# A diffusion trunk on one core: the first layer's feed-forward split into all latents, then the context, with the latents' projections behind the second sweep

## The chip, the cores and the metric

The kernel runs on one NeuronCore of a Trainium2 chip. The metric is the device time of one execution in microseconds (us). Engines are named as in the profile: PE is the matrix engine (PEld its weight loads), DVE the vector engine, ACT the scalar engine, POOL GpSimd, SP the engine that issues the weight transfers.

## The reference

Two layers over 1024 latent tokens and 256 context tokens, 1024 features, all in 32-bit floats. Layer 0 mixes tokens with a convolution module, layer 1 with grouped-query attention (16 query heads, 4 key heads, head size 64, normed q and k, rotary positions on latents). Each layer ends in a SwiGLU feed-forward of width 2816. Only latents are returned, so the last layer does not update the context.

```python
for i in range(DEPTH):                      # DEPTH = 2
    hx = rmsnorm(x, norm_g[i, 0]) * (1.0 + sc_x) + sh_x      # the same for ctx -> hc
    # i == 0: yx, yc = conv_module(hx), conv_module(hc)
    # i == 1: yx = attention over the keys of hx and hc
    x = x + g_x * rmsnorm(yx, norm_g[i, 1])
    fx = rmsnorm(x, norm_g[i, 2]) * (1.0 + scf_x) + shf_x
    x = x + gf_x * rmsnorm(swiglu(fx, ffn_w1[i], ffn_w3[i], ffn_w2[i]), norm_g[i, 3])
    # layer 0 alone does the last three lines for ctx, too
```

The shifts, scales and gates (`sh`, `sc`, `g`) come from six linear maps per layer of silu(c) for latents and of silu(c_ctx) for the context.

## The kernel before

Features lie on the 128 partitions, tokens in the columns. Tokens are cut into three pieces: C (256 context columns), L and R (512 latent columns each). A matmul of full precision is three matmuls on split halves: `mm3` (L154 to L156) multiplies weights' high part with both halves of the input and weights' low part with its high half. `wload` brings a weight tile of 512 KB into one of two landing buffers (`wr`), ACT casts the high part (`wh`, L131), DVE subtracts the low part (`wl`, L135; on POOL, L137, while `lo_dve` is 0); of each of these there are three buffers. Scratch comes from small rings: `sm` (3 buffers), `sb` (4), `acc` (2).

`ffn` walks over 22 tiles of the hidden width in groups of four (the last of two). For each, `up` loads the tiles of w1 and w3, multiplies all pieces of the call with them, and forms silu(a) * b (L646, L647) as two halves in a ring of five slots (`hrs`); one tile into the next group, `down` multiplies the group before with w2 and adds the result to y on DVE (L671). While the feed-forward is written down, `pump` takes steps of generators waiting in `bgq` (the background), each step with a cost, half a us of background for each nominal us of matmuls. The order thus written is a priority: within it each engine gets an instruction early or late as its inputs are expected, and each engine then runs its own list in order.

Around the change, the order before is:

- post-norms of the convolution (`pp`, a `post_pre`: sum of squares, scale, add to the residual, store as `x1d`, second norm into the halves `fv`) for C and L, then the convolution's last projection of R;
- a sweep of `ffn(0, ...)` over C and L; behind it R's `pp` and `mods`. The latter computes the modulation of layer 1: `mod_half` loads 112 chunks of 256 KB into four buffers and reduces each on DVE against one or two conditioning rows (L264). Its conditioning rows and buffers share one allocation (`HR`) with C's y;
- a sweep over R alone; behind it (`early`) the closing norms (`final`, which stores `x2d`) of C and L, layer 1's input norm of C, C's keys and values, and the input norm of L;
- `qkv` of L, `final` and `norm_in` of R, `qkv` of R. `qkv` projects K, V and four pairs of query tiles. `qk_pair` takes squares of both tiles of a pair on ACT, adds them on DVE (L715), sums each head by small matmuls (L719), takes reciprocal roots on DVE, rotates, splits and stores four parts (`ksd`, eight transfers for a K pair; `qsd`, four for a query pair);
- `attention`: a first pass of 16 units (4 key heads, 4 query blocks of L). A unit has scores (24 matmuls, L816), their scaling (L822) and exponentials, then transposes and the product with V (L834 to L841), one unit behind. R's query projections run in the background of its first units; meanwhile scores use one region of PSUM, and later two;
- the output projection of L with the second pass (R's query blocks) in the background, and layer 1's feed-forward.

## Time and profile before

| what | value |
|---|---|
| median of 3 runs | 3094.52 us (3092.87 to 3094.85) |
| profiled execution | 3094.26 us |
| its span, first to last instruction | 3092.0 us |
| mean granted PE clock | 0.969 |
| busy: PE, DVE, ACT, POOL | 2906.2, 1926.1, 1195.9, 264.6 us |
| HBM read, written | 289.76 MB, 41.81 MB |

In a row of a group of instructions stand line, engine, operation, output and inputs, shape and count; then busy us and the mean ns of one, then idle time of the engine before them with what ended it. A row of waits reads: who waited for whom, us in total, times, longest. A row of transfers has the count, KB each, and the median us from issue to landing. "in" names tensors in memory; lower-case and capital names are the program's tiles (`T` stands for T1 to T6).

### The profile page before, as it was taken

The page shows a single profiled execution, that of the slowest core. Times are in us where ns is not written, and L with a number is a line of the kernel's source. Part 1 is how long each engine was busy: PE and PEld are TensorE (multiplying, and loading weights), DVE is VectorE, ACT ScalarE, POOL GpSimd, SP SyncE. Part 2 cuts the span into 40 slices and gives each one's busy share as a digit, 9 for nine tenths or more (in the row PEclk, how much of TensorE's full clock was granted, in tenths as well). Part 3 has the DMA queues.
Part 4 walks back from the last instruction along what each step waited for, and adds up shares of the span by engine and source line. Part 5 has one row for each costly group of instructions (what it writes and reads, how often), then busy time and mean ns, then how long its engine had stood idle before and what let it go on. Part 6 is the DMA issues. An engine that isn't in the chain of part 4 may idle for free. (4 is left out here: it accounts for less than half of the span.)

```text
span 3092.0 us, 38855 instructions
## 1 busy us (share of the span) xinstructions
PE 2906.2 (94%) x14890; PEld 2416.0 (78%) x14890; DVE 1926.1 (62%) x3400; ACT 1195.9 (39%) x1880; POOL 264.6 (9%) x416
## 2 busy tenths in 40 slices
PE   7899969998999999999958899989999999999997
PEld 5788858887888887888846678767777778788886
DVE  5886777898533366433565899766566653743335
ACT  5222255421121134222333688645555543332222
POOL 0000001123100011000113211110000000100000
PEclk9999979999999999999979999989999999999999
DMA  6542424367312234333345311222222232443232
GB/s 234 148 126 68 134 87 140 140 198 234 127 62 65 65 116 137 109 96 96 118 145 154 96 64 43 86 79 75 67 83 78 67 121 95 150 131 95 95 95 75
DMA packets 143322, 339.58 MB, mean 110 GB/s; under 512 B 41888, under 2 KB 63392, under 8 KB 141984
## 3 DMA queue, kind: packets, MB, share of 16 engines
q1 hardware_dynamic: 76432, 221.94, 22.3%
q0 software_dynamic: 40592, 107.06, 11.1%
q10 hardware_dynamic: 26112, 8.10, 1.1%
q8 instruction: 117, 1.92, 0.3%
q14 instruction: 69, 0.57, 0.1%
HBM read 289.76 MB, written 41.81 MB: 107 GB/s over the span
## 5 line engine op out<-in xcount | busy, mean ns | idle before, releaser
L156 PE MATMUL ps<-T,wl 128*128 128x512 f32 (+1 forms) x2256 | 847.7, 377 | 22.8 <-DVE wl L135 22.8
L154 PE MATMUL ps<-T,wh 128*128 128x512 f32 (+1 forms) x2256 | 849.5, 377 | 13.1 <-ACT T L143 4.9
L155 PE MATMUL ps<-T,wh 128*128 128x512 f32 (+1 forms) x2192 | 822.3, 375 | 1.0 <-DVE T L146 0.7
L131 ACT CAST wh<-wr 128x1024 fp32r<-128x1024 f32 x348 | 365.4, 1050 | 1049.4 <-PE ps L155 774.6
L135 DVE TENSOR_TENSOR wl<-wr,wh 128x1024 fp32r<-128x1024 f32 x340 | 415.8, 1224 | 390.8 <-ACT wh L131 385.7
L156 PEld LDWEIGHTS ps<-T,wl 128*128 128x128 f32 x2256 | 430.3, 191 | 100.8 <-DVE wl L135 25.5
L154 PEld LDWEIGHTS ps<-T,wh 128*128 128x128 f32 x2256 | 430.4, 191 | 91.1 <-ACT T L143 6.4
L155 PEld LDWEIGHTS ps<-T,wh 128*128 128x128 f32 x2192 | 418.4, 191 | 74.7 <-DVE T L146 2.0
L155 PE MATMUL ps<-HS,wh 128*128 128x512 f32 (+1 forms) x784 | 306.4, 391 | 0.0
L838 DVE TENSOR_TENSOR T<-ps,T 128x512 fp32r<-128x512 f32 x320 | 216.8, 687 | 110.2 <-ACT T L837 108.9
L154 PE MATMUL ps<-HS,wh 128*128 128x512 f32 (+1 forms) x720 | 280.9, 392 | 0.0
L156 PE MATMUL ps<-HS,wl 128*128 128x512 f32 (+1 forms) x720 | 280.6, 390 | 0.0
L837 ACT CAST T<-ps 128x512 fp32r<-128x512 f32 x320 | 186.2, 586 | 182.9 <-PE ps L834 164.5
L834 PE MATMUL ps<-cst,T 128*128 128x128 f32 x1100 | 193.3, 277 | 17.7 <-DVE T L838 17.3
L671 DVE TENSOR_TENSOR T<-ps,T 128x512 f32<-128x512 f32 (+1 forms) x168 | 110.7, 664 | 146.0 <-PE ps L156 145.3
L822 DVE TENSOR_SCALAR_CACHE_REDUCE T<-ps,rq 128x1280 f32<-128x1280 f32 x110 | 169.9, 1545 | 29.2 <-PE ps L816 24.6
L834 PEld LDWEIGHTS ps<-cst,T 128*128 128x128 f32 x1100 | 133.8, 142 | 65.3 <-DVE T L838 45.5
L647 DVE TENSOR_TENSOR sm<-sm,ps 128x256 f32<-128x256 f32 (+1 forms) x88 | 54.5, 620 | 197.4 <-PE ps L156 197.3
L824 ACT ACTIVATE T<-T,mn 128x1280 f32<-128x1280 f32 x110 | 150.4, 1367 | 66.4 <-DVE T L822 64.5
L155 PEld LDWEIGHTS ps<-HS,wh 128*128 128x128 f32 x784 | 149.2, 190 | 29.0 <-DVE HS L146 0.2
L816 PE MATMUL ps<-KB,q 128*128 128x512 f32 (+1 forms) x576 | 144.6, 371 | 20.5 <-DMA KB<-ksd 13.0
L156 PEld LDWEIGHTS ps<-HS,wl 128*128 128x128 f32 x720 | 136.8, 190 | 27.7
(212 smaller groups left out, 4207.4 us busy)
## 6 DMA issues: line engine op xcount, KB each, us to landing
wr<-in_w SPq DMA_DIRECT2D x264, 512.0 KB, 3.5
wr<-in_pw SPq DMA_DIRECT2D x40, 512.0 KB, 3.6
raw<-in_wmodT POOLq DMA_DIRECT2D x56, 256.0 KB, 3.3
HR<-in_wmodT POOLq DMA_DIRECT2D x56, 256.0 KB, 3.3
wr<-in_wq SPq DMA_DIRECT2D x16, 512.0 KB, 7.5
qsd<-sb POOLq DMA_DIRECT2D x32, 256.0 KB, 9.9
q<-qsd POOLq DMA_DIRECT2D x32, 256.0 KB, 3.2
wr<-in_wo SPq DMA_DIRECT2D x16, 512.0 KB, 3.9
```

What stands on the lines that cost most here:

```text
L131: nc.scalar.copy(hi, raw)
L135: nc.vector.tensor_tensor(lo, raw, hi.bitcast(F32), op=ALU.subtract)
L154: nc.tensor.matmul(out[:, :n], lhsT=wh, rhs=xh, start=k == 0, stop=False)
L155: nc.tensor.matmul(out[:, :n], lhsT=wh, rhs=xl, start=False, stop=False)
L156: nc.tensor.matmul(out[:, :n], lhsT=wl, rhs=xh, start=False, stop=k == nk - 1)
L671: nc.vector.tensor_tensor(yd, out[:, :c1 - c0], yd, op=ALU.add)
L816: nc.tensor.matmul(sc[:, k0:k0 + w], lhsT=q[:, h, :], rhs=kt[:, p * TOK + k0:p * TOK + k0 + w], start=p == 0, stop=p == 1)
L822: nc.vector.tensor_scalar(out=pt, in0=sc, scalar1=rq[:, h:h + 1], scalar2=None, op0=ALU.mult, op1=ALU.min, accum_out=mn)
L824: nc.scalar.activation(pt, pt, AF.Exp, bias=mn, scale=-1.0, accum_out=sums[:, 0, h:h + 1])
L834: nc.tensor.transpose(tp[:, h * P:(h + 1) * P], Ps[h][:, j * P:(j + 1) * P], c["ident"])
L837: nc.scalar.copy(ph, tp)
L838: nc.vector.tensor_tensor(pl, tp, ph.bitcast(F32), op=ALU.subtract)
```

## The change

The first layer's feed-forward takes L and R in one sweep and C alone in the next. In the first (`late=True`), five up-steps of L run before R's first five, which load the same tiles of w1 and w3 again; from then on each tile serves both. C's first post-norm only scales, adds and stores; its sum of squares is taken in the background of the first sweep from a reload, and its norm is applied ahead of that sweep's last group (`hook`). `mods` has three landing buffers for its chunks instead of four. Behind the sweep of C stand, for L and then for R, the closing norm, the input norm and projections: all of L's, and K and V of R. After it come C's closing and input norm, three query pairs of R, C's keys and values, and the last query pair. Attention's first pass has no background any more and two score regions from the start. In `qk_pair` the small matmuls add both squares in PSUM.

```diff
@@ -567,8 +567,8 @@
         n = y.shape[-1]
-        m = 4 if xtag == "KB" and n > 256 else KT
-        xr = self.T(xtag, [P, m, n])
+        m = 4 if isinstance(xtag, str) and xtag == "KB" and n > 256 else KT
+        xr = self.T(xtag, [P, m, n]) if isinstance(xtag, str) else xtag
             nc.gpsimd.dma_start(xr[:, q % m:q % m + 2, :], xsrc[:, q:q + 2, c0:c0 + n])
@@ -607,11 +607,12 @@
             yield self.pace
-    def ffn(self, l, fs, ytags, htags, boxes, tanh=False, parts=1):
-        nc = self.nc
-        xs = [self.pairs(*f) for f, _ in fs]
+    def ffn(self, l, fs, ytags, htags, boxes, tanh=False, parts=1, late=False, hook=None):
+        nc = self.nc
+        xs = lambda j: self.pairs(*(fs[j][0] if isinstance(fs[j][0], tuple) else fs[j][0][0]))
         ns = [n for _, n in fs]
         hrs = [self.T(t, [P, GRP + 1, 2, n], F32R) for t, n in zip(htags, ns)]
@@ -621,20 +622,20 @@
         def cols(w, o=0):
-        def up(ft):
+        def up(ft, js):
             i = ft % (GRP + 1)
             w1 = self.wload(self.a["w1"][l, ft])
-            pas, pbs = [self.bank("mm") for _ in ns], []
-            for x, n, pa in zip(xs, ns, pas):
-                self.mm3(pa, cols(w1), x, KT, n)
+            pas, pbs = [self.bank("mm") for _ in js], []
+            for j, pa in zip(js, pas):
+                self.mm3(pa, cols(w1), xs(j), KT, ns[j])
             w3 = self.wload(self.a["w3"][l, ft])
-            for x, n in zip(xs, ns):
+            for j in js:
                 pbs.append(self.bank("mm"))
-                self.mm3(pbs[-1], cols(w3), x, KT, n)
-            slot[ft] = []
-            for n, pa, pb, hr in zip(ns, pas, pbs, hrs):
-                hh, hl = hr[:, i, 0, :], hr[:, i, 1, :]
-                slot[ft].append((hh, hl))
+                self.mm3(pbs[-1], cols(w3), xs(j), KT, ns[j])
+            for j, pa, pb in zip(js, pas, pbs):
+                n = ns[j]
+                hh, hl = hrs[j][:, i, 0, :], hrs[j][:, i, 1, :]
+                slot[ft, j] = hh, hl
                 sa, h = self.sm(n), self.sm(n)
                     nc.scalar.activation(sa, pa[:, :n], AF.Tanh, scale=0.5)
@@ -663,7 +664,7 @@
             for dd in range(2):
                 out = self.bank("mm")
-                self.mm3(out, cols(w, dd * G), lambda k: [v[:, c0:c1] for v in slot[fts[k]][j]], G, c1 - c0)
+                self.mm3(out, cols(w, dd * G), lambda k: [v[:, c0:c1] for v in slot[fts[k], j]], G, c1 - c0)
                 yd = y[:, d, c0:c1]
                     nc.scalar.copy(yd, out[:, :c1 - c0])
@@ -674,8 +675,12 @@
             for i, ft in enumerate(fts):
-                up(ft)
-                yield 48 * col
+                ups = [(ft, range(len(ns)))]
+                if late and ft <= GRP:
+                    ups = [(ft, (0,))] + [(f, (1,)) for f in range(ft + 1) if ft == GRP]
+                for f, js in ups:
+                    up(f, js)
+                    yield 48 * sum(ns[j] for j in js) / 2400
                 if i == 0 and g > 0:
                         w = w2(g - 1, d2)[0]
@@ -684,6 +689,8 @@
                         yield 6 * len(GROUPS[g - 1]) * col
         ws = []
+        if hook is not None:
+            hook()
         if len(ns) > 1:
         for j, n in enumerate(ns):
@@ -712,12 +719,12 @@
         nc.scalar.activation(s2, psO[:, :n], AF.Square)
         nc.scalar.activation(O, psO[:, :n], AF.Identity, scale=g[:, 1:2])
-        nc.vector.tensor_tensor(s1, s1, s2, op=ALU.add)
         ps = self.bank("st")
             with self.later():
-                nc.tensor.matmul(ps[:, 4 * j:4 * j + 4], lhsT=s1[:, j * P:(j + 1) * P], rhs=c["blk"],
-                                 start=True, stop=True)
+                for i, sq in enumerate((s1, s2)):
+                    nc.tensor.matmul(ps[:, 4 * j:4 * j + 4], lhsT=sq[:, j * P:(j + 1) * P], rhs=c["blk"],
+                                     start=i == 0, stop=i == 1)
         v = self.tiny([P, 16], "nv")[:, :4 * J]
                                 op0=ALU.mult, op1=ALU.add)
@@ -1002,21 +1009,25 @@
             pass
             pass
-        for b in ("C", "L"):
-            for _ in pp(b):
-                pass
+        def sink_C(k):
+            nc.gpsimd.dma_start(self.x1d[:, k, :CTX], yv["C"][0][0][:, k, :])
+        for _ in self.post(0, 1, *yv["C"][0], a["xT"], 0, segs_of(0, CTX), sink_C, "HR"):
+            pass
+        for _ in pp("L"):
+            pass
         for _ in self.pw2("R", tags["R"][0], sv["R"][0], yv["R"]):
         zv = {b: [] for b in PIECES}
+        preC = []
-            cr = room[:, 2048:4096].rearrange("p (s d) -> p s d", s=2)
-            raws = [room[:, o:o + 512] for o in (4096, 4608)]
-            raws += [self.sp.tile([P, 512], F32, tag="q", name="raw", bufs=2) for _ in range(2)]
+            room = self.T("KB", [P, 2560])
+            cr = room[:, :2048].rearrange("p (s d) -> p s d", s=2)
+            raws = [room[:, 2048:]] + [self.sp.tile([P, 512], F32, tag="q", name="raw", bufs=2) for _ in range(2)]
             self.cond_row(cr)
                 yield from self.mod_half(l, range(f0, 48), cr, raws, self.ps[:, 5, :])
@@ -1024,62 +1035,85 @@
             self.derive(1, (0,))
-        def rest_R():
+        def behind():
             yield from pp("R")
             yield from mods()
-        room = self.T("HR", [P, 5120])
-        self.bgq.append(rest_R())
-        for us in self.ffn(0, [(fv["C"][0], CTX), (fv["L"][0], 512)], (room[:, :2048].rearrange("p (k n) -> p k n", k=KT), "T5"), ("KB", "HS"),
-                           (zv["C"], zv["L"])):
+            x = self.T("KB", [P, KT, CTX])
+            nc.gpsimd.dma_start(x, self.x1d[:, :, :CTX])
+            acc = self.acc(CTX)
+            for k in range(KT):
+                self.sq_acc(acc, x[:, k, :], k)
+                yield 0.5
+            preC.append((x, self.stat(acc, CTX)))
+        def norm_C():
+            x, pb = preC[0]
+            fv["C"].append(self.halves("T2", "T2", CTX))
+            for k in range(KT):
+                self.apply(x[:, k, :], pb, 0, 2, segs_of(0, CTX), *fv["C"][0], k)
+        def before_last():
+            self.drain()
+            norm_C()
+        self.bgq.append(behind())
+        for us in self.ffn(0, [(fv["L"][0], 512), (fv["R"], 512)], ("T5", "T1"), ("HS", "HR"),
+                           (zv["L"], zv["R"]), late=True, hook=before_last):
+            self.pump(0.5 * us)
+        def final(l, y, src, dst, c0, c1, dcol, xtag, kind="st", eng=nc.gpsimd):
+            segs = segs_of(c0, c1)
+            def sink(k):
+                if dst is not None:
+                    eng.dma_start(dst[:, k, c0 - dcol:c1 - dcol], y[0][:, k, :])
+            yield from self.post(l, 3, y[0], y[1], src, c0 - (CTX if l else 0), segs, sink, xtag, kind)
+        hC, hL, hR = [], [], []
+        self.rq = [self.cp.tile([P, SEQ // P * 4], F32, tag=f"rq{t}", name=f"rq{t}") for t in range(NKV)]
+        qr = []
+        def early():
+            yield from final(0, zv["L"][0], self.x1d, self.x2d, *PIECES["L"], 0, "KB")
+            self.vst = self.T("HR", [P, NKV, NJ, P], F32R)
+            yield from self.norm_in(1, None, (None, "HS", "T6"), *PIECES["L"], hL, xt=zv["L"][0][0])
+            wk = self.T("T5", [P, 8, 512])
+            yield from self.qkv(hL[0], CTX, 512, wk)
+            yield from final(0, zv["R"][0], self.x1d, self.x2d, *PIECES["R"], 0, "KB")
+            yield from self.norm_in(1, None, (None, "HS", "T6"), *PIECES["R"], hR, xt=zv["R"][0][0])
+            qr.append(self.qkv(hR[0], CTX + 512, 512, wk))
+            for _ in range(5):
+                yield next(qr[0])
+            self.kub = self.T("KB", [P, 2 * TOK], F32R)
+            self.load_k(0, self.kub, CTX, TOK)
+        self.set_banks(mm=[0, 1, 2, 3], st=[5, 6], cv=[4, 7])
+        t3 = self.T("T3", [P, 2, KT, CTX])
+        self.bgq.append(early())
+        for us in self.ffn(0, [(fv["C"][0], CTX)], (t3[:, 0],), ("T4",), (zv["C"],),
+                           hook=self.drain):
             self.pump(0.5 * us)
...
-        def early():
-            yield from final(0, zv["C"][0], self.x1d, self.x2d, *PIECES["C"], 0, "KB")
-            yield from final(0, zv["L"][0], self.x1d, self.x2d, *PIECES["L"], 0, "KB")
-            yield from self.norm_in(1, None, (None, "T2", "T2"), 0, CTX, hC, xt=zv["C"][0][0])
-            self.vst = self.T("HR", [P, NKV, NJ, P], F32R)
-            self.rq = [self.cp.tile([P, SEQ // P * 4], F32, tag=f"rq{t}", name=f"rq{t}") for t in range(NKV)]
-            wk = self.T("KB", [P, 8, 256])
-            yield from self.qkv(hC[0], 0, CTX, wk, False)
-            yield from self.norm_in(1, None, (None, "T3", "T2"), CTX, CTX + 512, hL, xt=zv["L"][0][0])
-            self.wk = self.T("T5", [P, 8, 512])
-        self.set_banks(mm=[0, 1, 2, 3], st=[5, 6], cv=[4, 7])
-        self.bgq.append(early())
-        for us in self.ffn(0, [(fv["R"][0], 512)], ("T1",), ("HS",), (zv["R"],)):
-            self.pump(0.5 * us)
-        self.drain()
-        self.bgq.append(self.qkv(hL[0], CTX, 512, self.wk))
-        self.pump(7)
-        self.kub = self.T("KB", [P, 2 * TOK], F32R)
-        self.load_k(0, self.kub, 0, CTX + 512)
-        for _ in final(0, zv["R"][0], self.x1d, self.x2d, *PIECES["R"], 0, "T4", "cv"):
+        for _ in final(0, zv["C"][0], self.x1d, None, *PIECES["C"], 0, t3[:, 1], "cv"):
             pass
-        for _ in self.norm_in(1, None, (None, "T4", "T6"), CTX + 512, TOK, hR, xt=zv["R"][0][0], kind="cv"):
+        for _ in self.norm_in(1, None, (None, "T2", "T2"), *PIECES["C"], hC, xt=t3[:, 0], kind="cv"):
             pass
-        self.drain()
-        qr = self.qkv(hR[0], CTX + 512, 512, self.wk)
-        next(qr)
-        self.load_k(0, self.kub, CTX + 512, TOK)
-        for _ in range(5):
-            next(qr)
-        self.attention(final, qr)
-    def attention(self, final, qr):
+        for _ in range(3):
+            next(qr[0])
+        for i, _ in enumerate(self.qkv(hC[0], 0, CTX, self.T("T4", [P, 8, CTX]), False)):
+            if i == 0:
+                self.load_k(0, self.kub, 0, CTX)
+        for _ in qr[0]:
+            pass
+        self.attention(final)
+    def attention(self, final):
         nc, a, c = self.nc, self.a, self.c
         pr1 = self.T("T1", [P, 3, TOK])
-        prh = self.T("HS", [P, 4, TOK])
+        pr4 = self.T("T5", [P, 3, TOK])
+        pr5 = self.T("T4", [P, 3, TOK])
         ptt = self.T("T2", [P, 4, 2, 512], F32R)
         self.ptslot = self.si = 0
@@ -1093,28 +1127,15 @@
                     nc.gpsimd.dma_start(self.od[:, 2 * t:2 * t + 2, q * P:(q + 1) * P], st)
             return of
         beside = dict(mm=[0, 1], pt=[5], st=[6], av=[7])
-        alone = dict(pt=[5, 6], av=[7])
-        self.set_banks(**beside)
-        self.lo_dve = 0.0
-        self.sring = [TOK]
-        self.pring = [pr1[:, 0], prh[:, 0], pr1[:, 1], prh[:, 1], pr1[:, 2], prh[:, 2], prh[:, 3]]
-        self.rate = 0.8
+        self.set_banks(pt=[5, 6], av=[7])
+        self.sring = [0, TOK]
+        self.pring = [x[:, i] for i in range(3) for x in (pr1, pr5, pr4)]
         self.lav = 40
-        self.bgq.append(qr)
-        pr4 = None
-        for us in self.attn_stream(units, (self.kub, kbuf), dst(0), True):
-            if self.bgq:
-                self.pump(self.rate * us)
-            elif pr4 is None:
-                pr4 = self.T("T5", [P, 3, TOK])
-                self.pring = self.pring[:4] + [pr4[:, 0], pr4[:, 1], pr4[:, 2]] + self.pring[4:]
-                self.set_banks(**alone)
-                self.sring = [0, TOK]
-        self.lav = 40
-        self.lo_dve = 1.0
+        for _ in self.attn_stream(units, (self.kub, kbuf), dst(0), True):
+            pass
         self.set_banks(mm=[6], st=[6], pt=[5], av=[7])
```

1 line of the change is left out of this document (removed).

## The prediction

> **What bounds the kernel now.** I read the page first, then the windows by stage, then the waits and transfers of the stages that stand out.
>
> ```profile
> span 3092.0 us, 38855 instructions
> PE 2906.2 (94%) x14890; PEld 2416.0 (78%) x14890; DVE 1926.1 (62%) x3400; ACT 1195.9 (39%) x1880; POOL 264.6 (9%) x416
> PE   7899969998999999999958899989999999999997
> DVE  5886777898533366433565899766566653743335
> PEclk9999979999999999999979999989999999999999
> ```
>
> TensorE (PE) is the bound nearly everywhere; VectorE (DVE) comes close in places. So time can only be won where PE stands still. The windows tell where (stretch, length, then busy time and instruction count of PE, PEld, DVE, ACT, POOL, then granted clock, DMA share, GB/s):
>
> ```profile
> 560.00:717.00 157.00, 156.59 (x890) 138.28 (x891) 147.15 (x338) 58.66 (x93) 32.83 (x61) 0.98 0.50 166
> 717.00:795.00 78.00, 69.23 (x377) 60.63 (x376) 59.72 (x144) 12.23 (x17) 30.62 (x57) 0.93 0.75 243
> 1125.00:1515.00 390.00, 382.99 (x1726) 315.68 (x1725) 196.58 (x312) 123.89 (x171) 21.12 (x34) 0.99 0.37 117
> 1515.00:1683.00 168.00, 122.59 (x614) 104.25 (x613) 101.76 (x239) 56.52 (x87) 38.44 (x50) 0.85 0.50 139
> 1683.00:1760.00 77.00, 69.09 (x329) 53.75 (x328) 62.16 (x133) 40.58 (x63) 21.24 (x23) 0.94 0.45 119
> 880.00:920.00 40.00, 40.00 (x234) 35.45 (x233) 11.79 (x15) 7.94 (x11) 0.00 (x0) 1.00 0.19 61
> 1280.00:1320.00 40.00, 40.00 (x177) 32.91 (x176) 16.19 (x19) 9.75 (x12) 0.00 (x0) 1.00 0.28 93
> ```
>
> The last two rows give PE's pace without gaps: 40/177 = 0.226 us for a matmul of 512 columns; 40/234 = 0.171 for the even mix of 256 and 512 in the first sweep, so 0.116 for 256. Busy time hides short gaps, so I price work by count times pace and call what a stretch takes beyond it "lost". The stretch that the change rebuilds begins with the first sweep and ends with the last score of attention's first pass:
>
> ```profile
> 560.40 1.01 PE L154 MATMUL ps<-T,wh 128*128 128x512 f32 x2 [4.15 <-ACT T L358]
> L816 PE MATMUL ps<-T,q x192: 277/393/483, 1776.7 to 1951.7; 128*128 128x512 f32 x128, 128*128 128x256 f32 x64
> ```
>
> From 560 to 1952 are 1391 us: the sweep over context and left latents (C, L) to 1125, that over the right latents (R) to 1515, a hole with the projections of L and R's K and V around R's closing norm to 1683, then attention with R's query projections beside its first units. In the hole the matmuls are K of L and R (96 of 512 columns, 21.7 us), both V (192 of 256, 22.3) and L's queries (192 of 512, 43.4): 87 us in 168, so 81 lost. What is waited for there:
>
> ```profile
> ACT wh L131 <- DMA wr<-in_wq: 47.8, 5, 12.8
> POOL KB L795 <- DMA ksd<-sb: 18.5, 2, 16.6
> PE ps L719 <- DVE sm L715: 16.7, 4, 6.3
> PE ps L156 <- DVE wl L135: 12.9, 2, 10.9
> PEld ps L816 <- DMA KB<-ksd: 12.7, 1, 12.7
> ```
>
> Weights that come late, head sums that wait for a DVE add, and K's round trip through memory.
>
> **The change, part by part.** The large matmuls stay the same in number; what moves is which run beside which.
>
> *Start.* C's first post-norm loses its statistics and its apply, which stood on DVE ahead of L's; the first up-projections need L alone. The 4.15 us of idle ahead of 560.4 should go and a little more: 5 off.
>
> *First sweep, L with R.* 22 x 48 up and 22 x 24 down matmuls, 1584 for each half: 2 x 1584 x 0.226 = 716. Five up-steps of L run before R's catch up, which loads w1 and w3 of these five twice: 10 loads on SP, 10 casts on ACT, 10 subtractions on DVE (1.22 each, 12 us), under 54 us of L's matmuls and beside R's post-norm (40 passes of 0.69 to 0.75 and two statistics, some 33 us of DVE). DVE ran at 94% from 560 to 717 with PE full, so that covers; without it, it would cost its 12.
>
> The modulation reductions run behind this sweep as before, but through three landing buffers instead of four:
>
> ```profile
> DVE ps L264 <- DMA HR<-in_wmodT: 10.5, 7, 2.3
> raw<-in_wmodT POOLq DMA_DIRECT2D x29, 256.0 KB, 3.8
> L264 DVE CUSTOM_DVE_ANT_0 ps<-raw,HR 128x512 f32<-128x512 f32 x80 | 55.8, 698 | 8.3 <-DMA raw<-in_wmodT 6.4
> ```
>
> The last 64 loads serve one reduction each. From 717 to 795 some 57 came in 78 us, 1.37 each, set by their landing; 377 PE instructions ran where 456 fit, so 13 us were lost. A buffer's round is the landing of 3.8, the reduction of 0.7 and some 0.4 of issue and read-out: 4.9 over three buffers is 1.63 each, 0.26 x 64 = 17 more. DVE takes its instructions in order, so weight splits and feed-forward products queue behind these waits. Bounds: 8 (steps of 21.7 us of matmuls instead of 16.4 hide more) and 43. I take 28, near 13 + 17, less a little for the wider steps.
>
> *Second sweep, C alone, with the projections behind.* C costs 1584 x 0.116 = 184. Beside it K of L and R 21.7, both V 22.3, L's queries 43.4. Together 271 us of matmuls, the same that were paid before. What DVE must do in that time:
>
> ```profile
> L135 DVE TENSOR_TENSOR wl<-wr,wh 128x1024 fp32r<-128x1024 f32 x340 | 415.8, 1224 | 390.8 <-ACT wh L131 385.7
> L345 DVE TENSOR_TENSOR acc<-acc,sb 128x512 f32<-128x512 f32 x119 | 81.7, 687 | 12.8 <-ACT sb L344 11.0
> L353 DVE SCALAR_TENSOR_TENSOR sb<-T,col,ps 128x512 f32<-128x512 f32 x56 | 39.3, 741 | 9.0 <-PE ps L333 7.8 <-issue 1.3
> L737 DVE TENSOR_TENSOR T<-T 128x512 f32<-128x512 f32 x10 | 8.0, 804 | 15.0 <-ACT T L713 15.0
> L647 DVE TENSOR_TENSOR sm<-sm,ps 128x256 f32<-128x256 f32 x22 | 9.2, 418 | 9.9 <-PE ps L156 9.9
> ```
>
> 82 weight splits (44 of w1 and w3, 22 of w2, 16 of projections) x 1.22 = 100; C's products, splits, sums and squares, 91 x 0.42 = 38; final and input norms of L and R, 78 x 0.72 = 56, with four statistics, some 9; six pairs of 8.5 to 10 (eight passes of 0.69 to 0.8, the reciprocal roots) = 54; V 3. That is 260 in 271 of PE: as tight as 560 to 717, and tighter in the two norm stretches. So some is lost. Lower bound: the R sweep, 1584 x 0.226 + 96 x 0.116 = 369 in 390, 21 lost, 6%; here 16. Upper: the hole lost 81 over five pairs; six like that, 97. C's matmuls fill gaps and the wait for L715 (16.7 of the 81) goes, so I lean low: 42.
>
> *Head sums on PE.* Each pair drops one DVE add (0.74) and doubles its small matmuls:
>
> ```profile
> L715 DVE TENSOR_TENSOR sm<-sm 128x512 f32<-128x512 f32 x10 | 7.4, 744 | 3.7 <-ACT sm L712 3.7
> L719 PE MATMUL ps<-cst,sm 128*128 128x4 f32 x84 | 13.2, 279 | 17.2 <-DVE sm L715 17.2
> 1590.17 1.68 PE L719 MATMUL ps<-cst,sm 128*128 128x4 f32 x8 [4.21 <-DVE sm L715]
> ```
>
> 84 records more. Eight took 1.68 us at a slow clock, 0.2 each: 17 at the most; nothing where PE waits anyway. I take 8, the middle. Both squares now stay in the three-deep scratch until PE has read them, and a product of C's feed-forward may wait for one; that lies within the second sweep's bounds.
>
> *After the sweeps.* C's closing and input norm, three of R's query pairs beside them, C's K and V, the fourth pair: 192 x 0.226 + 96 x 0.116 = 54.5 us of matmuls. Attention waits for C's K to be stored and reloaded. Lost, at least: that round trip, 12.7 above, less what the fourth pair hides, some 8; at most the hole's ratio (81 on 87), 50. I take 26, just under the middle: C's chains are half as wide, but nothing else is left to fill with.
>
> *Attention's first pass* runs alone, with two score regions from the start. The score row above has units 4 to 15 in 175 us, 14.6 each, the pace without projections beside. 15 x 14.6 = 219, and 7 for the first unit, which has only scores: 226. On POOL its query loads no longer queue behind R's query stores. C's eight stores of the second stream fall away; they were hidden. Eight subtractions go from POOL to DVE, counted above or under the tail's loss.
>
> *Turns.* 0.226 and 0.116 are rounded down and leave out the statistics' small matmuls; the R sweep has 24 of these. 5 in all.
>
> *Sum:* -5 + 716 + 28 + 271 + 42 + 8 + 54.5 + 26 + 226 + 5 = 1371.5 against 1391: 20 less. From the profiled execution's 3094.26 (0.3 under the median of 3094.52): 3074.
>
> **A rule against the trace.** In the hole the weights landed late beside the stores:
>
> ```profile
> wr<-in_w SPq DMA_DIRECT2D x264, 512.0 KB, 3.5
> wr<-in_wq SPq DMA_DIRECT2D x16, 512.0 KB, 7.5
> ksd<-sb POOLq DMA_DIRECT2D x16, 256.0 KB, 15.0
> qsd<-sb POOLq DMA_DIRECT2D x32, 256.0 KB, 9.9
> L131 ACT CAST wh<-wr 128x1024 fp32r<-128x1024 f32 x348 | 365.4, 1050 | 1049.4 <-PE ps L155 774.6 <-issue 108.8 <-DMA wr<-in_wq 47.8
> ```
>
> 7.5 us instead of 3.5 at the median, and 12.8 of waiting at the longest. The Trainium skill's page "DMA: Bandwidth & Descriptors" (Queues, rings and completion order) says that each engine takes turns between the queues that hold work, packet by packet. By that rule a load beside one busy store queue takes at most about twice as long, 7.0, and the trace agrees at the median, not at its longest.
>
> **The rivals.**
> *Slower: weight supply bounds the second sweep.* C uses a tile up in 24 x 0.116 = 2.8 us where R took 5.4, and there are two landing buffers. A buffer is held for landing, cast (1.05) and subtraction (1.22): 5.8 us at a landing of 3.5, so 2.9 a tile; 9.8 at 7.5, so 4.9. At 4.9 the 82 tiles take 402 where I have 271 + 42 + 5 = 318 with the sums: 84 more, 3158. It makes the kernel slower from 344 / 82 = 4.2 a tile. For it: six pairs store in this sweep, 8 MB, and the wait for in_wq is the hole's longest. Against: eight stores of a K pair, 0.7 apart, take some 20 us at 15.0, four of a query pair some 13 at 9.9: 2 x 20 + 4 x 13 = 92, under a third of the sweep, which gives 3.5 a tile, 287, below my 318. Queueing on DVE, at 96%, could lift it. As a case: 3105 to 3158, centre 3120.
> *No change: the pairs carry their cost with them.* Each pair writes its halves into four scratch buffers that come free only when its stores have landed, and the norms use the same buffers. If a pair in the sweep loses 10.5 us of the hole's 16 instead of 7, the sweep loses 62 instead of 42: 3094.
> *Faster still: the cover holds.* DVE at 94% with PE full (560 to 717) says that it can. With 16 lost in the sweep and 8 in the tail: 44 less than forecast, 3030; half of that is as likely.
>
> **How the numbers follow.** The forecast, 3074 (own range 3054 to 3087): 0.42. Cover holds: 0.16. No change: 0.14. Weight supply: 0.28. A change within 0.2%, 6 us, can't be told from none here. So faster 0.58, same 0.14, slower 0.28. From 3030 to 3125 lie the forecast, the no-change case, three quarters of the fast case and half of the slow one, 0.82.
>
> **What would show it.** First sweep: some 745 us, with PE's gaps where L264 waits for its loads. Second: about 320, DVE near 80%, no gap of PE over 5 us; wrong if casts waiting for in_w and in_wq lead. Tail: R's query pairs between C's norms, one wait for ksd; wrong if it lasts over 100 us. Attention: 14.6 us a unit from the second on. Head sums: L719's successor waits for ACT instead of DVE.

## The result and the profile after

The changed kernel takes 3146.8 us (median of 4 runs, 3146.4 to 3153.9) where the kernel before, on the same chip, takes 3094.7: a ratio of 1.017 (95% interval 1.015 to 1.019). It is slower by 52 us where I forecast 20 us less. The profiled execution spans 3145.4 us.

First the head of the page of the changed kernel, its DVE and clock rows of 40 slices included, against the lines shown of before:

```profile
span 3145.4 us, 39000 instructions
PE 2936.8 (93%) x14974; PEld 2438.2 (78%) x14974; DVE 1927.1 (61%) x3405; ACT 1204.9 (38%) x1890; POOL 246.5 (8%) x403
PE   7999869999999999998898699998999999999997
DVE  5886776995523223764666599866666653753335
PEclk9999979999999999998999799998999999999999
```

PE has 84 instructions more (the second head-sum matmuls) and 30 us more of busy time; DVE has the same busy time as before. So PE waited, and worked more slowly where it did. The windows by stage say where (columns as before):

```profile
560.00:717.00 157.00, 156.08 (x693) 127.45 (x692) 145.88 (x330) 59.56 (x85) 32.51 (x61) 1.00 0.56 180
717.00:815.00 98.00, 88.90 (x371) 71.37 (x370) 58.28 (x141) 12.64 (x18) 31.45 (x58) 0.97 0.63 197
815.00:1306.00 491.00, 489.17 (x2137) 400.17 (x2136) 165.53 (x230) 94.71 (x134) 4.26 (x6) 1.00 0.18 55
1306.00:1678.00 372.00, 324.53 (x2214) 303.38 (x2213) 231.09 (x445) 146.97 (x218) 39.95 (x61) 0.92 0.54 165
1678.00:1787.00 109.00, 77.53 (x392) 65.47 (x391) 67.10 (x196) 38.81 (x66) 17.88 (x26) 0.82 0.42 122
1787.00:2009.00 222.00, 213.57 (x1259) 172.17 (x1257) 199.29 (x324) 179.91 (x303) 30.53 (x49) 0.99 0.17 55
```

The three upper rows are the first sweep (L with R), which begins at 559.4 and ends at 1305.9. Then come the second sweep (C alone, with projections behind), the tail, and attention's first pass. Against the forecast's parts:

| part | forecast, us | trace, us | off by |
|---|---|---|---|
| start of the first sweep | 555.4 | 559.4 | +4 |
| first sweep | 744 | 746 | +2 |
| second sweep, with turns | 318 | 372 | +54 |
| tail and attention's first pass | 80.5 + 226 | 109 + 222 | +24 |
| head sums, as a term of their own | 8 | (within the rest) | -8 |

That is 76 of the 77 us by which the last score of the first pass (2008.8; 1951.7 before) came later than forecast. The second pass and the second layer's feed-forward behind it took 4 us less than before. The cut between the tail and attention at 1787 is mine: the first eight score matmuls already run between 1774.8 and 1781, so the two are best read together, 331 us against 306.5.

Some of what the second sweep waited for (us in total, times, longest; GpSimd's own waits are left out), and then its transfers (median us to landing is the last column):

```profile
DVE wl L135 <- ACT wh L131: 100.5, 36, 10.1
ACT wh L131 <- DMA wr<-in_w: 79.9, 29, 11.7
ACT wh L131 <- PE ps L155: 45.7, 19, 5.5
ACT wh L131 <- DMA wr<-in_wq: 17.2, 4, 9.3
PE ps L156 <- DVE wl L135: 14.5, 11, 5.6
PE ps L154 <- ACT wh L131: 10.3, 5, 4.6
```

```profile
wr<-in_w SPq DMA_DIRECT2D x62, 512.0 KB, 4.0
ksd<-sb POOLq DMA_DIRECT2D x16, 256.0 KB, 13.3
qsd<-sb POOLq DMA_DIRECT2D x16, 256.0 KB, 10.8
```

ScalarE waits 97 us for weights to land, VectorE waits for ScalarE's casts, TensorE waits for both: the row that the prediction named as its disproof ("wrong if casts waiting for in_w and in_wq lead"). Yet DVE is busy for 231 of 372 us, 62%, far below the 80% that I expected.

### The profile page after: what moved, and what is told of

The parts are those of the page before. It is cut to its first block, busy times and chain, and to the rows that moved or that the text cites. A ratio compares the mean times of both kernels' runs of the same rounds, so it can differ in the third digit from the quotient of the medians.

```text
span 3145.4 us, 39000 instructions
## 1 busy us (share of the span) xinstructions
PE 2936.8 (93%) x14974; PEld 2438.2 (78%) x14974; DVE 1927.1 (61%) x3405; ACT 1204.9 (38%) x1890; POOL 246.5 (8%) x403
## 5 line engine op out<-in xcount | busy, mean ns | idle before, releaser
L155 PE MATMUL ps<-T,wh 128*128 128x512 f32 (+1 forms) x2368 | 877.8, 371 | 1.4 <-DVE T L146 1.0
L154 PE MATMUL ps<-T,wh 128*128 128x512 f32 (+1 forms) x2272 | 843.9, 373 | 21.6 <-DVE T L672 8.1
L135 DVE TENSOR_TENSOR wl<-wr,wh 128x1024 fp32r<-128x1024 f32 x356 | 435.0, 1222 | 441.6 <-ACT wh L131 438.7
L155 PEld LDWEIGHTS ps<-T,wh 128*128 128x128 f32 x2368 | 458.8, 194 | 76.2 <-DVE T L146 2.4
L154 PEld LDWEIGHTS ps<-T,wh 128*128 128x128 f32 x2272 | 439.2, 194 | 93.5 <-ACT wh L131 14.1
L154 PE MATMUL ps<-HS,wh 128*128 128x512 f32 (+1 forms) x704 | 276.6, 394 | 9.1 <-ACT wh L131 9.1
L155 PE MATMUL ps<-HS,wh 128*128 128x512 f32 (+1 forms) x608 | 236.7, 390 | 0.0
L672 DVE TENSOR_TENSOR T<-ps,T 128x512 f32<-128x512 f32 (+1 forms) x208 | 126.8, 616 | 156.1 <-PE ps L156 154.8
L829 DVE TENSOR_SCALAR_CACHE_REDUCE T<-ps,rq 128x1280 f32<-128x1280 f32 x128 | 197.6, 1544 | 21.6 <-PE ps L823 16.9
L841 PEld LDWEIGHTS ps<-cst,T 128*128 128x128 f32 x1280 | 150.0, 141 | 69.5 <-DVE T L845 43.6
L831 ACT ACTIVATE T<-T,mn 128x1280 f32<-128x1280 f32 x128 | 175.0, 1367 | 60.9 <-DVE T L829 58.8
L154 PEld LDWEIGHTS ps<-HS,wh 128*128 128x128 f32 x704 | 134.0, 191 | 37.3 <-ACT wh L131 10.6
L648 DVE TENSOR_TENSOR sm<-sm,ps 128x512 f32<-128x512 f32 (+1 forms) x88 | 54.4, 618 | 164.9 <-PE ps L156 164.6
```

The lines of the kernel that those rows point to most:

```text
L135: nc.vector.tensor_tensor(lo, raw, hi.bitcast(F32), op=ALU.subtract)
L154: nc.tensor.matmul(out[:, :n], lhsT=wh, rhs=xh, start=k == 0, stop=False)
L155: nc.tensor.matmul(out[:, :n], lhsT=wh, rhs=xl, start=False, stop=False)
L672: nc.vector.tensor_tensor(yd, out[:, :c1 - c0], yd, op=ALU.add)
L829: nc.vector.tensor_scalar(out=pt, in0=sc, scalar1=rq[:, h:h + 1], scalar2=None, op0=ALU.mult, op1=ALU.min, accum_out=mn)
L831: nc.scalar.activation(pt, pt, AF.Exp, bias=mn, scale=-1.0, accum_out=sums[:, 0, h:h + 1])
```

## The experiments

Each is an edit of the changed kernel (or of what is named), timed against the kernel before on the same chip. Line numbers in the rows are those of each kernel, a few lines on from the changed one's.

### Four landing buffers in the second sweep

```diff
-        raw = self.wp.tile([P, 1024], F32, tag="wr", name="wr", bufs=2)[:, :n]
+        raw = self.xraw[self.xi % len(self.xraw)]
+        self.xi += 1
+        if raw is None:
+            raw = self.wp.tile([P, 1024], F32, tag="wr", name="wr", bufs=2)
+        raw = raw[:, :n]
...
+        t3f = t3[:, 1].rearrange("p k n -> p (k n)")
+        self.xraw = [None, t3f[:, :1024], None, t3f[:, 1024:]]
```

Two of the four are still those of the pool, the other two lie in the idle half of tile T3.

> The changed kernel with four landing buffers in place of two for the weight tiles of the second sweep (the two more are the half of tile T3 that lies idle until the sweep's end); nothing else. If the supply of weight tiles sets the second sweep (82 tiles, each landing buffer held for load, cast and subtraction, 372 us in all against 271 of matmuls), the sweep falls to 290 to 320 us and the time to 3070 to 3100. If the tiles are late because the low parts are made late in VectorE's queue, a landing buffer more only lets tiles wait longer in SBUF: sweep 365 to 375, time 3140 to 3150.

Measured: 3100.5 us, ratio 1.0018 (1.0006 to 1.0030), 46 less than the changed kernel. The window of its second sweep, and two of its waits:

```profile
1307.00:1627.00 320.00, 305.73 (x2217) 288.62 (x2216) 229.50 (x443) 145.37 (x217) 42.79 (x65) 0.98 0.61 188
```

```profile
ACT wh L137 <- PE ps L161: 83.5, 42, 7.4
ACT wh L137 <- DMA T<-in_w: 13.4, 3, 7.3
```

320 us instead of 372, and casts now wait for PE to free a buffer (83.5) instead of for a landing. Both numbers are at the edge of what was expected for supply, and far from the other case. So the ring of two landing buffers held the sweep. It took time in two ways: PE's idle time falls from 47 to 14 us, and the same matmuls take 305.7 us of busy time instead of 324.5, at a granted clock of 0.98 instead of 0.92. The whole gains 46 and not 52, because the tail and attention's first pass take 340 us here instead of 331; why was not followed up.

### Half of the low parts on GpSimd

`self.lo_dve = 0.5` for the second sweep.

> The changed kernel with every second low-part subtraction of the second sweep on GpSimd in place of VectorE. If VectorE's queue makes the low parts late, the sweep loses 20 to 50 us: time 3100 to 3130. If the landing of the tiles sets the sweep, nothing is gained (3140 to 3155), and it can get slower, since GpSimd also issues the stores of K and q and waits up to 69 us for their scratch buffers: a subtraction behind such a wait holds its landing buffer as long (3150 to 3250).

Measured: 3186.8 us, ratio 1.029 (1.027 to 1.031), 40 slower. Its second sweep takes 406 us:

```profile
POOL wl L137 <- ACT wh L131: 203.2, 32, 19.0
ACT wh L131 <- DMA wr<-in_w: 99.7, 31, 12.5
```

Taken from VectorE, the 40 subtractions are slower: they take 2.45 us each on GpSimd, against 1.22 on VectorE in the changed kernel, and a landing buffer is held 9.8 us on average instead of 9.1. Longer holds of the same two buffers cost more, which fits supply. It is no clean test of VectorE's queue, since each subtraction moved also became slower.

### The context's weights not loaded

The `dma_start` of the context's tiles are left out; cast and subtraction read one resident tile. The page has 208 loads of `in_w` instead of 274: 66 are gone, not the 62 of the expectation, which are those issued within the sweep's window.

> The changed kernel with the context's feed-forward weights left out: each of its 62 tiles is cast and split from one tile that lies in SBUF, so 62 loads of 0.5 MB fall away in the second sweep, while casts, subtractions and matmuls stay. If the loads (their latency, and the two landing buffers) are what is late, the sweep falls to 280 to 310 us and the time to 3060 to 3090. If the casts and subtractions in their engines' order are, the sweep stays above 350 and the time above 3125.

Measured: 3095.6 us, ratio 1.0006 (0.9994 to 1.0018).

```profile
1309.00:1625.00 316.00, 303.95 (x2217) 286.86 (x2217) 230.06 (x444) 145.10 (x217) 41.37 (x63) 0.98 0.32 89
```

316 us with no load for the context at all, while every cast and subtraction stays: without the ring, these two in their engines' order do not hold the sweep above 316. Four buffers come within 4 us of that, so they hide nearly all of the loading. The 45 us above the floor of 271 that stay are as large as the loss and the turns that I forecast (42 + 5); what they consist of was not tried. Sweep and time both missed what was expected, 280 to 310 and 3060 to 3090; the tail keeps its own loss.

### The projections behind the sweep, not beside it

`self.bgq.append(early())` moved behind the context's sweep.

> The changed kernel with the latents' norms, projections and stores run after the context's sweep in place of behind it. It shows what the two cost apart. If the weight ring is slowed by the stores of K and q that share the DMA engines, the context's sweep alone runs at the quiet hold of some 5.8 us over two buffers, 2.9 us a tile, 62 tiles in 180 to 200 us, which is its matmul floor of 184. If the ring itself is too slow for 256 columns, it takes 240 to 260 us alone too. The projections alone then need 87 us of matmuls and what their chains expose, 150 to 250 us; the time is 3150 to 3250.

Measured: 3170.4 us, in one run only. The windows of the context's sweep alone and of the projections alone, then the sweep's loads:

```profile
1307.00:1508.00 201.00, 195.97 (x1592) 193.31 (x1591) 111.92 (x158) 86.43 (x125) 0.00 (x0) 0.98 0.54 171
1508.00:1741.00 233.00, 162.77 (x819) 137.35 (x819) 158.25 (x399) 80.71 (x131) 42.66 (x65) 0.80 0.46 129
```

```profile
wr<-in_w SPq DMA_DIRECT2D x62, 512.0 KB, 3.5
```

Alone, the sweep needs 201 us for 184 of matmuls (180 to 200 expected): two buffers nearly suffice when nothing runs beside it. Taken tile by tile from the records (issue, landing, start of cast, end of subtraction), a landing buffer is held 5.98 us on average here, 62 tiles, and 9.13 in the changed kernel, 81 tiles. The 3.15 more are 1.43 of landing (4.99 instead of 3.56), 0.80 of waiting before the cast and 0.93 of waiting before the subtraction. In the changed kernel the waits before casts are 73 us in all: 33 end when TensorE frees one of the three cast buffers, 20 pass with ScalarE at other instructions, and the rest is mostly idle time in front of those. Of the 79 us before subtractions VectorE is at other instructions for 65.

9.13 / 2 x 82 is 374, the sweep took 372. That must come out wherever a freed buffer is loaded again at once, here after 0.03 us: it tells where a buffer's time goes. That the ring sets the pace is told by the two runs before, with four buffers and without the loads.

### K stored once

Attention loads the same K rows into the lower and the upper 64 partitions; here they are stored once and loaded twice.

```diff
-            for r in (i % 2, i % 2 + 2):
+            r = i % 2
...
+        for p in (0, 64):
...
+                                   self.ksd[t, :64, :, c0:c1])
```

> The changed kernel with K stored once in place of twice (the upper 64 partitions of what attention loads are a copy of the lower 64, so two loads from the one copy give the same): 2 MB of stores fewer in the second sweep and 0.5 MB fewer in the tail. If the weight tiles of the second sweep are late because the stores beside them share the DMA engines (tiles beside stores were held 11 to 16 us, quiet ones 5.6 to 6), the sweep falls by 10 to 20 us: time 3127 to 3137. If the ring of two is too slow anyhow, 3142 to 3148.

Measured: 3141.5 us, ratio 1.016 (1.013 to 1.019): 5 less, within the intervals and in neither theory's favour. The sweep falls to 369 us only, and the mean hold from 9.13 to 9.04. So this quarter of the stores, 2 of 8 MB, is worth next to nothing; what the stores cost as a whole was not tried. The records of the changed kernel show that landings are late beside GpSimd's transfers: 44 tiles with none of these under way landed in 3.6 us on average, 37 beside at least one in 6.6. Landing is 1.43 of the 3.15 us by which a hold grew.

### Four modulation buffers

`room` gets 3072 columns in place of 2560, `raws` a fourth buffer from it.

> The changed kernel with four buffers in place of three for the modulation weights that are reduced behind the first sweep. If the ring of three makes TensorE wait in the first sweep (between 717 and 815 us it is busy 88.9 of 98 us), 5 to 12 us come back: 3135 to 3142. If those waits are of other work, nothing changes: 3145 to 3150.

Measured: 3123.9 us, ratio 1.010 (1.008 to 1.012), 23 less, twice what was expected. The waits of the reductions from 717 us on, the changed kernel's first and then its own, and its window:

```profile
DVE ps L264 <- DMA KB<-in_wmodT: 20.8, 14, 3.7
DVE ps L264 <- DMA raw<-in_wmodT: 17.1, 27, 2.0
```

```profile
DVE ps L264 <- DMA KB<-in_wmodT: 12.0, 11, 2.1
```

```profile
717.00:815.00 98.00, 93.70 (x404) 76.46 (x403) 65.36 (x149) 20.87 (x34) 28.29 (x52) 0.98 0.62 200
```

In 98 us PE runs 404 instructions where the changed kernel runs 371. The first sweep ends at 1290.9 instead of 1305.9: the fourth buffer is worth 15 us there, where the prediction charged 17 for its loss. The other 8 came after attention's first pass and are taken up at the end.

### Seven scratch buffers for the pairs

Three 512-column buffers in the idle part of T4's room join the pool of four for what a pair stores.

> The changed kernel with seven scratch buffers in place of four for what the pairs of the projections store (K and q, high and low parts), from the second sweep to the first attention unit; the three more are the part of tile T4's room that the context's sweep leaves idle. The landing buffers stay two. If ScalarE and VectorE are held in the tail by stores that have not landed (the trace of the changed kernel with four landing buffers has ScalarE waiting up to 6.5 us for a store of q, and the context's V weights late by 16 us behind that), the tail shrinks by 12 to 20 us and the second sweep by 0 to 15: time 3115 to 3135. If weight supply alone is at fault, 3143 to 3150.

Measured: 3150.1 us, ratio 1.019 (1.017 to 1.021): no gain. Waits of the tail, of the changed kernel and then of this one:

```profile
PE ps L155 <- DVE wl L135: 12.2, 1, 12.2
ACT sb L143 <- DMA qsd<-sb: 11.2, 2, 5.6
DVE sb L146 <- DMA qsd<-sb: 8.3, 2, 7.4
```

```profile
PE ps L162 <- DVE wl L142: 8.4, 1, 8.4
PE ps L161 <- ACT wh L138: 6.4, 1, 6.4
DVE sb L153 <- DMA qsd<-sb: 6.2, 1, 6.2
```

The waits for stores shrink, but TensorE still waits for the context's weights, 8.4 + 6.4 us instead of 12.2. The rival "the pairs carry their cost with them", in its form with scratch buffers, falls.

### Head sums: the add back on VectorE, and the change alone

> The changed kernel with the squares of a pair added on VectorE again and one head-sum matmul per block, as before. The prediction took 8 us (0 to 17) for the head sums on TensorE: by that the time is 3139 (3130 to 3147). If VectorE's queue is the tighter one in the sweep, it gets slower, 3150 to 3155.

> The kernel before with only the head sums moved to TensorE (two matmuls per block in place of the add on VectorE). The prediction's 8 us would give 3103 (3094 to 3112). If the small matmuls fit into gaps that TensorE has there, 3092 to 3097.

> The fastest kernel so far (four landing buffers from the second sweep through the tail, four modulation buffers, two q pairs ahead) with a pair's squares added on VectorE and one head-sum matmul per block, as before the change. If the doubled head sums cost TensorE the 8 us of the prediction: 3041 to 3047. If they lie beside other work: 3049 to 3055. If VectorE's add is the dearer one: 3056 to 3065.

Measured: the changed kernel with VectorE's add 3153.1 (1.017 to 1.022, no different from 1.017 of the changed one); the kernel before with the head sums on TensorE 3096.7, ratio 1.0015 (1.0004 to 1.0025), some 4 us more; the fastest kernel (below) with the add 3051.3 against 3052.3 without. So the head sums on TensorE cost -6, 4 and 1 us, where I took 8; only the 4 is clear of the noise, and its interval reaches from 1 to 8.

```profile
L726 PE MATMUL ps<-cst,sm x168: 167/253/375, 1386.1 to 1779.8; 128*128 128x4 f32 x168
  ACT sm L719: 14.5, 5
  ACT sm L718: 9.7, 4
```

In the changed kernel the head sums wait for ScalarE's squares instead of VectorE's add, as forecast: a wait stays, its releaser changes.

### Pieces together

Four landing and four modulation buffers; then seven scratch buffers as well; then K stored once as well.

> The changed kernel with four landing buffers in the second sweep and four modulation buffers in the first, nothing else. The two pieces lie in different stretches, so their gains (46 and 23 us, of which 15 by the first sweep's end) should add: 3075 to 3085. If the modulation's gain behind the first attention pass was chance, 3085 to 3090.

> As the one with four landing and four modulation buffers, and the pairs' scratch ring of seven as well. Alone the seven buffers gave nothing, though ScalarE and VectorE waited for stores; if that was because the weight tiles were late in any case, 8 to 16 us come back now in the tail: 3062 to 3075. If the order of VectorE's queue in the tail holds the context's V weights back, no difference: 3075 to 3085.

> As the one with four landing, four modulation and seven scratch buffers, and K stored once in place of twice. If stores beside the weight loads still matter there, 5 to 12 us less than that kernel; if the deeper rings hide them, within 4 us of it.

Measured: 3080.1 us (ratio 0.9958, 0.9945 to 0.9972), 3085.7 (0.9974, 0.9961 to 0.9988) and 3079.8 (0.9956, 0.9943 to 0.9969). The first two pieces add. Scratch buffers and K's stores give nothing clear of the intervals here: the second run is 6 us above the first, the third back at it. With these two rings deepened, the change is 13 us (0.4%) faster than the kernel before; 8.5 of these lie in the last stretch, the second layer's feed-forward, which no edit touches (see the end).

### The tail

From the kernel with four landing and four modulation buffers: the landing buffers kept through the tail; two pairs of R's queries ahead of the context's K and V instead of three (`for _ in range(2): next(qr[0])`); both; both with K stored once; both with one pair ahead.

> The kernel with four landing and four modulation buffers, and the four landing buffers kept through the tail, for the context's K and V weights. If a late load holds the context's V and the second square of its K, the V gap (16.6 us) shrinks by 5 to 10 and the time falls to 3070 to 3076. If the queues of VectorE and ScalarE hold them, within 3 us of 3080.

> The kernel with four landing and four modulation buffers, with two of the right half's q pairs ahead of the context's K and V in place of three, and two behind them. If those pairs hold VectorE's and ScalarE's queues, the V gap falls by 8 to 16 us, and the pair behind covers part of the 9.8 us in which the first scores wait for K: 3060 to 3072. If they are needed as cover for the context's norms, TensorE idles there instead and nothing is gained: 3078 to 3088.

> Both: four landing buffers in the tail, and two q pairs ahead in place of three. If each cause has its own part, 3055 to 3068; if one of them alone decides, the better of the two within 4 us.

> As the one with both, and K stored once in place of twice. The first scores wait for the chain of K's last stores and its load (9.8 us): with four stores in place of eight 3 to 5 us less than that kernel; if the load alone is what takes the time, within 2 us.

> The fastest kernel so far with one q pair ahead of the context's K and V and three behind. If VectorE's and ScalarE's queues still hold the context's K and V, 4 to 8 us less: 3044 to 3049. If TensorE runs out of cover in the context's norms, 5 to 15 us more: 3057 to 3068.

Measured: 3071.9 (0.9935, 0.9912 to 0.9958), 3069.6 (0.9922, 0.9898 to 0.9947), 3052.3 (0.9873, 0.9850 to 0.9896), 3053.6 (0.9873, 0.9852 to 0.9895), 3055.1 (0.9872, 0.9853 to 0.9891). Alone the two edits take 8 and 11 us, together 28, more than was expected (3055 to 3068); each single time is uncertain by some 7 us, so that 28 exceeds the sum is not shown. The other two edits add nothing: the time with one pair ahead lies between its two expectations. The window of tail and first pass, and the tail's two longest waits of PE, first of the kernel with neither edit, then of that with both:

```profile
1614.00:1954.00 340.00, 293.26 (x1651) 241.14 (x1650) 268.49 (x523) 221.39 (x373) 48.55 (x76) 0.92 0.26 78
```

```profile
PE ps L162 <- DVE wl L141: 16.3, 1, 16.3
PE ps L829 <- DMA KB<-ksd: 9.6, 1, 9.6
```

```profile
1612.00:1924.00 312.00, 285.41 (x1647) 233.45 (x1646) 267.08 (x519) 219.51 (x368) 48.48 (x75) 0.97 0.27 85
```

```profile
PE ps L327 <- DVE acc L351: 8.6, 1, 8.6
PE ps L829 <- DVE T L835: 7.5, 2, 7.4
```

Both long waits are gone, the late low part of V's weights and K's reload, which R's pairs now cover. 312 us is near the 306.5 that I forecast for these two stages, and 19 less than the 331 of the changed kernel.

## Why the prediction was wrong, point by point

*Start and first sweep: right.* Forecast to end at 1299.4, ended at 1305.9. The sweep took 746 us against 716 + 28. Of the 30 lost, a fourth modulation buffer gives 15 back, where 17 had been charged for its loss. The start gained 1 us instead of 5: the wait before the first up-projection went, but R's second projection ended later.

*Second sweep, the step that failed.* The term was 42 us lost; with turns 318 in all, against 372. Its bounds came from stretches in which TensorE uses a tile up in 5.4 us, and held no term for supply. That stood among the rivals, at 0.28 and 3105 to 3158, and this rival happened: 372 / 82 tiles is 4.5 us a tile, beyond the 4.2 from which I said that it decides. Four landing buffers bring the sweep to 320. So 318 was right for a sweep that is supplied, and supply costs 52. That alone gives 3074 + 52 = 3126; the measured 3146.8 lies in the rival's range with the tail's loss on top, which the rival did not hold. I argued supply away by an average: stores fill a third of the sweep, which gave 3.5 us a tile. The average held for the landings: 4.99 of landing, the cast and the subtraction make 7.26, 3.6 a tile and 298 us, still below 318. It left out that each buffer also waits before its cast and its subtraction, 1.88 us a tile, mostly behind other instructions on VectorE and ScalarE, and in part for TensorE to free a cast buffer. I had named queueing on VectorE and given it no price. That two buffers store no lead, so that early tiles do not make up for late ones, may add to it; this is argued and was not tried by itself.

The Trainium skill's page "DMA: Bandwidth & Descriptors" (Queues, rings and completion order) says that each engine takes turns between its queues packet by packet, from which I had estimated at most about twice the quiet landing beside one busy store queue, 7.0 us. Here 14 of 81 tiles took longer, the longest 13.6; the measurement goes beyond that estimate. All 14 had at least four of GpSimd's transfers beside them, and in 6 of them, up to 10.9 us, no other weight load was in flight when they were issued; why they took so long stays open.

*VectorE at 96% in the sweep: wrong.* 260 us were forecast in 271; 231 were used in 372, and 229.5 in the 320 of the supplied sweep. So its work was counted 29 us too high, and the engine was not full: what mattered was its order: subtractions stood behind other instructions for 65 us, and each held its landing buffer meanwhile.

*Head sums: over-sized.* 8 forecast, -6 to 4 measured, mostly within the noise.

*Tail, the second step that failed.* 26 us lost were forecast; 109 - 54.5 is 54, and the 109 are beyond the 100 that I had named as the sign of being wrong. My bounds reached 50, but I took just under the middle, since "C's chains are half as wide". What counted was the order: three pairs of R's queries stand ahead of the context's K and V on ScalarE and VectorE, and both engines wait in them for stores. Two rows of ScalarE, two of VectorE and then one of TensorE in the changed kernel's timeline show it (start, duration; in brackets the idle time before and what ended it):

```profile
1730.40 0.62 ACT L143 CAST sb<-T 128x512 fp32r<-128x512 f32 x1 [5.60 <-DMA qsd<-sb]
1738.70 0.62 ACT L143 CAST sb<-T 128x512 fp32r<-128x512 f32 x1 [5.59 <-DMA qsd<-sb]
```

```profile
1742.81 0.69 DVE L146 TENSOR_TENSOR sb<-T,sb 128x512 fp32r<-128x512 f32 x1 [7.43 <-DMA qsd<-sb]
1743.71 1.22 DVE L135 TENSOR_TENSOR wl<-wr,wh 128x1024 fp32r<-128x1024 f32 x1
```

```profile
1744.99 0.58 PE L155 MATMUL ps<-wl,T 128*128 128x256 f32 x1 [12.19 <-DVE wl L135]
```

V's first weight landed at 1716.7 and was cast at 1717.0; its low part was made at 1743.7, behind the pair that waits for its stores. Four landing buffers and two pairs ahead end this; alone they give 8 and 11 us, together 28. Which part of it is the waiting for stores and which the pairs' own work was not separated: with seven scratch buffers the low part comes at 1739.3, and the next weights land later in turn.

*Attention's first pass: right.* Units 4 to 15 run from 1834.3 to 2008.8, 14.5 us each (14.6 forecast). The 222 against 226 hang on the cut at 1787.

*The other rivals.* "Cover holds" needed the supply to hold and fell with it.

With both failed steps mended and the fourth modulation buffer back, the change comes to 3052.3 us, 1.3% under the kernel before and below the forecast of 3074. Not all of that is the change's: in the stretch that it rebuilds, the last score of the first pass comes at 1924.2 instead of 1951.7, 27.5 us earlier (20 forecast), and 10 more lie in the second layer's feed-forward, which no edit touches. The kernel before was not tried with deeper rings; whether it has room for them stays open.

## What to carry to other kernels

When a change halves what the matrix engine does per weight tile, first work out the time that a landing buffer is held, queueing on the casting engines included, and divide by the number of buffers; if that is near the new use per tile, the ring has to become deeper in the same change. Idle halves of tiles whose life begins later serve well as landing buffers. And in a tail, look at what stands ahead of the critical chain in the order of the helper engines: cover for the matrix engine is work for them too. Here moving one of three pairs behind the chain gave 11 us, and moving a second gave nothing more.

## What the runs showed of the hardware that was not expected

*A gap costs twice.* After TensorE's gap of 12.19 us in the changed kernel, matmuls of 256 columns start 0.21 us apart, and 0.12 apart from 1748.76 on:

```profile
1745.37 0.41 PE L156 MATMUL ps<-wh,T 128*128 128x256 f32 x1
1745.58 0.41 PE L154 MATMUL ps<-wh,T 128*128 128x256 f32 x1
```

```profile
1748.76 0.28 PE L154 MATMUL ps<-wh,T 128*128 128x256 f32 x1
1748.88 0.28 PE L155 MATMUL ps<-wl,T 128*128 128x256 f32 x1
```

That is nearly half speed for the first 3.6 us, and the clock column of the windows (0.82 in the tail, 0.92 in the sweep) agrees. The Trainium skill's page "TensorE: Matmul & The Clock Gate" (Part 1: The HAM clock gate) says that an idle window of about 3.4 us halves the clock until activity has lasted as long. The trace agrees for this gap. Of the 52 us that supply cost the sweep, 19 are slower matmuls, which a sum of waits alone leaves out; the clock column fits, with 0.08 x 372 = 30 us of full speed not granted against 0.02 x 320 = 6, part of it while TensorE stood idle.

*One pace, two values.* In the second layer's feed-forward, which no edit touched, matmuls ran 261 to 60 us in the kernel with four landing buffers and 266 with the fourth modulation buffer as well, both at a granted clock of 1.00:

```profile
2923.50:2983.50 60.00, 60.00 (x261) 48.80 (x261) 22.48 (x25) 15.80 (x19) 0.00 (x0) 1.00 0.30 97
```

```profile
2906.70:2966.70 60.00, 60.00 (x266) 49.69 (x265) 22.94 (x26) 15.94 (x20) 0.00 (x0) 1.00 0.31 97
```

The part after the second pass's last score takes 589 to 594 us in the traces of all ten kernels with the larger room, and 597 to 601 in the ten others, the kernel before (601) among them. This is where the other 8 us of the fourth modulation buffer come from, and 10 of the 42 us by which the fastest kernel beats the kernel before. Why the pace differs was not tried; that enlarging the room moved other tiles is only a guess.
